# A list scheduler's cost table, the store of the gate rows and the loads of w_ada, changed together in a two-layer attention / DeltaNet step

## The chip, the cores and the metric

One NeuronCore of one Trainium2 chip runs the whole step. The metric is the device time of one execution in microseconds, taken as the median of several executions. The engines are called PE (matrix multiply), DVE, ACT and POOL (elementwise work) and SP (the engine that issues the DMAs of this kernel, all into one queue).

## What is computed

Two layers, each with 256 context tokens and 1024 latent tokens of width 1024, all in float32:

```
mod = silu(cond) @ w_ada + b_ada;  shift, scale, gate = split(mod, 3)
h   = rmsnorm(x) * (1 + scale) + shift
z   = h @ w_in                       # q, kv latents, k_pe, gates, q/k/v of DeltaNet, a, b
o_a = attention(q, k, v) * silu(g_a) # 8 heads, keys = tokens (+ 256 cached)
o_b = rmsnorm(delta_fwd + delta_bwd) * silu(g_b)  # 4 heads, chunked gated delta rule
x   = x + gate * (concat(o_a, o_b) @ w_out)
```

A final rmsnorm gives the outputs; the compressed keys, the rotary keys and the final DeltaNet states are outputs too. `gate` is one row of 1024 numbers for context tokens and one for latent tokens, in each layer.

## The kernel before

**Order of the work.** The kernel's Python code holds a planner, the class `Sched`. The work is written as some forty generators ("threads": projection weights, projection matmuls, evacuation, DeltaNet heads, attention heads, adaLN, output). Every instruction a thread asks for becomes an `Op` with an engine, a planned duration (`Eng.ns`, line 314) and the tiles that it reads and writes. `Sched.run` (line 104) always takes the op that could start first by its own clocks, and at equal time the thread with the lower number in `PR`. So the planner's durations decide the order of the instructions on each engine, and they decide nothing else: on the chip each engine runs its own list in that order, and a wait at the head of a list holds up all that is behind it. `keep_warm` (line 177) puts filler matmuls on the tile `spare` (line 406) into planned gaps of PE.

**What the planner believes.** A float32r matmul of n columns takes 0.4219 n ns (216.0 ns for 512), a plain float32 one four times that. The second and later of several matmuls into fewer than 65 partitions take 20 ns, and going back to a full-width matmul costs 85 ns. A DMA occupies SP for 450 ns, starts 1100 ns later, moves 360 bytes per ns, one DMA after the other, and its reader can start 931 ns after that (`LAT`, line 68; `Op.emit`, line 263).

**The w_ada pieces.** `ada` (line 452) makes one of the modulation vectors, half of it at a time: eight pieces of w_ada of 128 by 512, four matmuls with a two-column stationary operand each into `adap`, four copies into `msb`, a transpose into `modtp`, an add of the bias. The first four halves come from `init_thread`; the eight later ones (64 pieces of 256 KB) come from `ada_thread` (line 810), which loads each piece into the one buffer `wa` and then multiplies it, beside the layer-0 projection.

**The gate rows.** At the end of the two gate vectors (`s == 2 and half`, line 476) two DMAs write `modG` [128 partitions, 8] to the DRAM rows `gate_d[l, c]`, with the partition as the fastest index of the row: 1024 elements of 4 bytes each. `load_gate` (line 1675) reads the rows back much later, broadcast over partitions.

**The inverse of the DeltaNet chunks.** For each head `inv_thread` (line 1055) inverts the 32 by 32 diagonal blocks on DVE, writes them by four DMAs through `diag` (line 965; 1280 runs of 128 bytes each) into `wz_d` and `ai_d`, reads whole 128 by 128 blocks back into `wd` and `tt` (`rows`), and multiplies them on PE into `ph`.

**The seam of the two layers.** `mm_thread` makes the output projection tile by tile (ten tiles of 128 tokens); `fin(t)` (line 1679) stores the new x of a tile, normalises it, transposes it and splits it for layer 1 (`emit_h`, line 492).

Of the kernel before, what the change touches and what calls it, by code (L numbers as in the profile page):

```python
# [8 lines left out]
F32 = mybir.dt.float32  # L9
F32R = mybir.dt.float32r  # L10
# [4 lines left out]
DRAM = bass.MemoryType.DRAM  # L15

P = 128
DM = 1024
KD = DM // P
# [37 lines left out]
class Sched:  # L57
# [25 lines left out]
    half = False  # L83
# [135 lines left out]
class Op:  # L219
    def __init__(self, call, eng, ns, outs, ins):  # L220
        self.call, self.eng, self.ns = call, eng, ns
        self.outs, self.ins = [Sched.span(x) for x in outs], [Sched.span(x) for x in ins]
        self.thread = Sched.active
        self.half = outs[0].start_partition() if eng == "PE" and int(outs[0].shape[0]) <= 64 else None
        self.names = {n for n, _ in self.outs}
# [37 lines left out]
    def emit(self):  # L263
        s = self.start()
        if self.eng == "PE":
            if self.half:
                self.ns = 20
            elif Sched.half and self.half is None:
                s += 85
            Sched.half = self.half is not None  # L270
        e = s + self.ns
        if self.eng == "PE":
            Sched.keep_warm(s)
            Sched.busy.append((s, e))
        if self.eng == "D":
            e = Sched.bw = max(s + 1100, Sched.bw) + self.ns
        Sched.clk[self.eng] = s + 450 if self.eng == "D" else e
        e = int(e) * 8 + Sched.CODE[self.eng]
# [12 lines left out]


class Eng:
# [5 lines left out]
    def __getattr__(self, name):  # L299
        f = getattr(self.eng, name)  # L300

        def g(*a, **k):
            aps = [x for x in list(a[1:]) + list(k.values()) if hasattr(x, "start_partition")]
            acc = k.get("accum_out")
            outs = [a[0]] if acc is None else [a[0], acc]
            op = Op(lambda: f(*a, **k), self.key, self.ns(name, a, k, aps), outs, [x for x in aps if x is not acc])  # L306
            if Sched.active is None:
                op.emit()
            else:
                Sched.active.q.append(op)  # L310

        return g

    def ns(self, name, a, k, aps):
        size = lambda t: int(np.prod(t.shape[1:]))
        n = size(a[0])
        if self.key == "D":
            return int(np.prod(a[0].shape)) * 4 / 360
        if self.key == "PE":
            if name == "transpose":  # L320
                return 109
            if n == 1:
                return 214
            f = 0.4219 * (1 if a[2].dtype == F32R else 4)
            return f * max(n, min(int(a[1].shape[1]), 128))
# [42 lines left out]
def body(tc, I, O):  # L368
# [83 lines left out]
    def ada(l, s, half, load, msb):  # L452
# [23 lines left out]
        if s == 2 and half:  # L476
            for c in range(2):
                SY.dma_start(gate_d[l, c].rearrange("(k p) -> p k", p=P), modG[:, l, :, c])
# [49 lines left out]
    def mixer(l, hhl):  # L528
# [179 lines left out]
        def evac_conv(j, h, b, c0, n, ps):  # L708
# [11 lines left out]
            y = wp.tile([P, 520], F32, tag="yc", name="yc", bufs=2)[:, : e - a]  # L720
# [3 lines left out]
            th = wp.tile([P, 520], F32, tag="thc", name="thc", bufs=1)  # L724
# [85 lines left out]
        def ada_thread():  # L810
            yield "gdn"

            def load(l, k, c0):
                w = wp.tile([P, 512], F32, tag="wa", name="wa", bufs=1)
                SY.dma_start(w, I["w_ada"][l, k * P : (k + 1) * P, c0 : c0 + 512])
                yield 0
                return w

            msb = wp.tile([P, P], F32, tag="msb", name="msb", bufs=1)
            G.memset(msb, 0.0)  # L820
            for ll, s in ((0, 2), (1, 0), (1, 1), (1, 2)):
                for half in range(2):
                    yield from ada(ll, s, half, load, msb)
# [150 lines left out]
        def gram_thread(h):  # L974
# [24 lines left out]
            k2 = ap.tile([P, NT], F32, tag="k2", name="k2", bufs=3)  # L999
# [11 lines left out]
            n2 = ap.tile([P, NT], F32, tag="n2", name="n2", bufs=3)  # L1011
# [4 lines left out]
            bp = ap.tile([P, 2, NT], F32, tag="bp", name="bp", bufs=3)  # L1016
            kdb = ap.tile([P, 2, NT], F32, tag="kdb", name="kdb", bufs=3)
# [343 lines left out]
        def rope():  # L1361
# [6 lines left out]
            for g in range(2):  # L1368
                w = wp.tile([P, 520], F32, tag="thc", name="wpe", bufs=1)[:, 0:512].rearrange("p (a b) -> p a b", a=2)
                SY.dma_start(w, I["w_qpe"][l, g])  # L1370
                yield 0
                for b, (c0, n) in enumerate(BLK):
# [7 lines left out]
                    A = wp.tile([P, 520], F32, tag="yc", name="ra", bufs=2)[:, :n]  # L1380
                    if b == 0:
                        S.copy(A, pts[0][:, :n])
                    else:
                        B = wp.tile([P, 520], F32, tag="yc", name="rb_", bufs=2)[:, :n]
# [294 lines left out]
        def fin(t):  # L1679
# [3 lines left out]
            if l < DEPTH - 1:  # L1683
                if t in (0, 2, 6):
                    if t:
                        yield f"fin{t-1}"
                    alloc_h(*nxt)
# [169 lines left out]
```

## Time and profile before

| what | value |
|---|---|
| median of 3 runs | 2316.05 us (2313.68 to 2320.44) |
| the profiled execution's own time | 2314.35 us |
| its span, first to last instruction | 2312.4 us |
| granted PE clock, mean over the span | 0.976 |
| busy PE, DVE, ACT, POOL | 2123.5, 1461.7, 773.1, 830.1 us |
| moved by DMA | 306.9 MB in 369,808 packets, of which 92,624 under 512 bytes |

Busy time of PE counts the filler matmuls too. All instructions have the line of one helper (L306, the call of `Op`), so groups are told apart by their tiles: `ph<-wd,tt` is a matmul that reads `wd` and `tt` and writes `ph`. A plain float32 matmul stands in the profile as two records. The idle time behind an arrow is that of the engine just before the instruction, and the arrow names what ended it. The granted clock has two levels, 1.00 (2.4 GHz) and 0.50 (1.2 GHz).

### The profile page before, as it was taken

Reading aid. Unit: us, or ns where it says so; the run is one execution under the profiler, and the core shown is the slowest. Engines: PE = TensorE matmul, PEld = TensorE weight load, DVE = VectorE, ACT = ScalarE, POOL = GpSimd, SP = SyncE. Lnnn points to the kernel's source line nnn. Section 1 sums busy time; section 2 is a strip of 40 time slices with the busy share of each in tenths; the row PEclk is TensorE's granted clock in tenths of the full one; section 3 lists DMA queues with packets and bytes.
Section 4 is the critical chain, followed back from the end, with each engine's and each line's share of the span. In section 5 each row is a group of like instructions: output and inputs, shape, how many; then the busy total and the mean of one; then the engine's idle time right before and its main releaser. Section 6 shows DMA issues by size and latency. Waiting matters only on the chain. (4 is left out here: it accounts for less than half of the span.)

```text
span 2312.4 us, 35225 instructions
## 1 busy us (share of the span) xinstructions
PE 2123.5 (92%) x12230; PEld 1536.0 (66%) x12230; DVE 1461.7 (63%) x3085; ACT 773.1 (33%) x2118; POOL 830.1 (36%) x757
## 2 busy tenths in 40 slices
PE   8988998699988999999999899979988899999998
PEld 5666776578656654555777778867866666555576
DVE  5846367666775675654676556786767566565454
ACT  4242142323223445443222313331332234544311
POOL 2332123231523248355331421452152223844521
PEclk9999999899999999999999999999999999999999
DMA  7475666675844322101423545646685431310143
GB/s 264 129 188 140 194 199 192 141 219 149 273 137 123 99 87 68 27 23 39 151 97 96 154 141 158 184 137 194 188 240 154 119 88 50 102 45 23 39 151 109
DMA packets 369808, 306.90 MB, mean 133 GB/s; under 512 B 92624, under 2 KB 308112, under 8 KB 369376
## 3 DMA queue, kind: packets, MB, share of 16 engines
q1 hardware_dynamic: 369632, 304.66, 44.9%
q8 instruction: 97, 1.59, 0.3%
q14 instruction: 79, 0.65, 0.1%
HBM read 199.11 MB, written 105.46 MB: 132 GB/s over the span
## 5 line engine op out<-in xcount | busy, mean ns | idle before, releaser
L306 PE MATMUL zp<-hh,wh 128*128 128x512 f32 (+2 forms) x1128 | 425.5, 377 | 1.3 <-ACT qtp L306 0.9
L306 PE MATMUL zp<-hh,wl 128*128 128x512 f32 (+2 forms) x1128 | 421.4, 374 | 4.7 <-POOL wl L306 2.6
L306 PE MATMUL zp<-hl,wh 128*128 128x512 f32 (+2 forms) x1128 | 421.2, 373 | 2.7 <-POOL hl L306 1.5
L306 POOL TENSOR_TENSOR wl<-wr,wh 128x512 fp32r<-128x512 f32 (+1 forms) x114 | 158.7, 1393 | 399.3 <-DVE wh L306 247.1
L306 ACT ACTIVATE pe<-sp 128x512 f32<-128x512 f32 (+1 forms) x352 | 200.9, 577 | 246.0 <-PE sp L306 228.0
L306 DVE TENSOR_REDUCE at<-pm 128x1 f32<-128x512 f32 (+1 forms) x336 | 214.2, 682 | 103.9 <-PE pm L306 103.2
L306 POOL TENSOR_TENSOR pe<-pe,pe 128x1024 f32<-128x1024 f32 x96 | 229.8, 2394 | 90.2 <-DVE pe L306 64.7
L306 PE MATMUL sp<-at 97*128 97x512 f32 (+1 forms) x704 | 241.1, 408 | 1.4 <-ACT pe L306 0.9
L306 PEld LDWEIGHTS zp<-hh,wl 128*128 128x128 f32 (+1 forms) x1128 | 215.6, 191 | 37.8 <-issue 4.0
L306 PEld LDWEIGHTS zp<-hl,wh 128*128 128x128 f32 (+1 forms) x1128 | 215.7, 191 | 37.0 <-issue 4.3
L306 PEld LDWEIGHTS zp<-hh,wh 128*128 128x128 f32 (+1 forms) x1128 | 215.8, 191 | 36.2 <-issue 5.5
L306 PE MATMUL po<-pe,vv 128*64 128x512 f32 (+1 forms) x768 | 183.7, 561 | 3.2 <-ACT pe L306 2.4
L306 PEld LDWEIGHTS sp<-at 97*128 97x128 f32 x704 | 123.2, 190 | 89.1 <-issue 58.1
L306 POOL TENSOR_SCALAR kpt<-ktok,kdb 128x128 f32<-128x128 f32 x160 | 113.5, 722 | 91.6 <-DMA kp_d<-kpt 81.0
L306 PE MATMUL sp<-at,at 97*128 97x512 f32 (+1 forms) x352 | 137.9, 392 | 0.0
L306 PE MATMUL pm<-at 96*128 96x512 f32 (+1 forms) x416 | 128.0, 381 | 4.7 <-DMA ti<-ai_d 2.1
L306 DVE TENSOR_TENSOR pe<-pe,pe 128x256 f32<-128x256 f32 (+1 forms) x64 | 74.8, 1171 | 79.6 <-POOL pe L306 56.5
L306 PE MATMUL wop<-woh,oh 128*128 128x512 f32 x288 | 115.0, 399 | 0.9 <-DVE oh L306 0.9
L306 PE MATMUL wop<-woh,ol 128*128 128x512 f32 x288 | 114.1, 396 | 1.5 <-POOL ol L306 1.5
L306 PE MATMUL wop<-wol,oh 128*128 128x512 f32 x288 | 114.5, 398 | 0.0
L306 PEld LDWEIGHTS pm<-at 96*128 96x128 f32 x416 | 70.9, 189 | 58.4 <-ACT pe L306 17.9
L306 DVE TENSOR_TENSOR wtmp<-blk,W 104x31 f32<-104x31 f32 (+15 forms) x248 | 104.0, 419 | 7.0 <-POOL W L306 2.7
(264 smaller groups left out, 3895.1 us busy)
## 6 DMA issues: line engine op xcount, KB each, us to landing
wr<-in_w_main SPq DMA_DIRECT2D x116, 256.0 KB
ai_d<-ai SPq DMA_DIRECT2D x80, 256.0 KB
ti<-ai_d SPq DMA_DIRECT2D x160, 128.0 KB
wa<-in_w_ada SPq DMA_DIRECT2D x64, 256.0 KB
kqv_d<-yc SPq DMA_DIRECT2D x48, 256.5 KB
kq<-kqv_d SPq DMA_DIRECT2D x16, 641.0 KB
rb<-grow_d SPq DMA_DIRECT2D x80, 128.0 KB
kp_d<-kpt SPq DMA_DIRECT2D x80, 128.0 KB
```

Of the source, the lines that this page charges most:

```text
L306: op = Op(lambda: f(*a, **k), self.key, self.ns(name, a, k, aps), outs, [x for x in aps if x is not acc])
```

## The change

It gives the planner other durations: a float32r matmul 0.4545 ns per column (232.7 ns for 512), a plain float32 one 1.676; 92 ns for the change from full-width matmuls to ones with at most 64 output partitions and 200 ns back; 8 ns for a neighbour in the same bank; a DMA by its runs of contiguous bytes (`descriptors`), at 160 ns a run under 16 bytes and 8 + b/26 ns a run of b bytes otherwise (9 more under 512 bytes), divided by 16; and SP busy for at least one ns per run. The gate rows are transposed on PE and copied by ACT to 16 partitions of 128, and one DMA stores them. The later w_ada pieces are loaded by a thread of their own into two buffers, and the multiplying thread waits for flags. Small buffers lose a copy or six columns to make room. Each `fin(t)` waits for the one before it, where three did.

```diff
-                self.ns = 20
-            elif Sched.half and self.half is None:
-                s += 85
-            Sched.half = self.half is not None
+            n = self.outs[0][0]
+            if (self.half is None) != (Sched.half is None):
+                s = max(s, Sched.clk.get("PE", 0.0) + (92 if Sched.half is None else 200))
+            if self.half is not None:
+                if Sched.half not in (None, (n, self.half)) and Sched.half[0] == n:
+                    self.ns = 8
+            Sched.half = None if self.half is None else (n, self.half)
...
-        Sched.clk[self.eng] = s + 450 if self.eng == "D" else e
+        Sched.clk[self.eng] = s + self.issue if self.eng == "D" else e
...
+            if self.key == "D":
+                op.issue = max(450, self.descriptors(a[0], a[1])[0])
...
-            return int(np.prod(a[0].shape)) * 4 / 360
+            m, b = self.descriptors(a[0], a[1])
+            return m * (160 if b < 16 else 8 + b / 26 + (9 if b < 512 else 0)) / 16
...
-            f = 0.4219 * (1 if a[2].dtype == F32R else 4)
-            return f * max(n, min(int(a[1].shape[1]), 128))
+            if a[2].dtype == F32R:
+                return 0.4545 * max(n, 128)
+            if int(a[0].shape[0]) <= 32 and n < 128:
+                return 0.84 * n
+            return 1.676 * max(n, min(int(a[1].shape[1]), 128))
...
         if s == 2 and half:
-            for c in range(2):
-                SY.dma_start(gate_d[l, c].rearrange("(k p) -> p k", p=P), modG[:, l, :, c])
+            yield 0
+            pt = yield from bank("modtp")
+            PE.transpose(pt[0 : 2 * KD, 0:P], modG[:, l].rearrange("p k c -> p (k c)"), ident)
+            S.copy(msb[0 : 2 * KD, :], pt[0 : 2 * KD, 0:P])
+            free(pt)
+            SY.dma_start(gate_d[l].rearrange("c (k p) -> k c p", p=P), msb[0 : 2 * KD, :])
...
-            y = wp.tile([P, 520], F32, tag="yc", name="yc", bufs=2)[:, : e - a]
+            y = wp.tile([P, 514], F32, tag="yc", name="yc", bufs=2)[:, : e - a]
...
-            def load(l, k, c0):
-                w = wp.tile([P, 512], F32, tag="wa", name="wa", bufs=1)
-                SY.dma_start(w, I["w_ada"][l, k * P : (k + 1) * P, c0 : c0 + 512])
-                yield 0
-                return w
...
+            def loads():
+                for ll, s, half in jobs:
+                    for k in range(KD):
+                        i = len(wq)
+                        if i >= 2:
+                            yield f"au{i-2}"
+                        w = wp.tile([P, 512], F32, tag="wa", name="wa", bufs=2)
+                        c0 = s * DM + half * 512
+                        SY.dma_start(w, I["w_ada"][ll, k * P : (k + 1) * P, c0 : c0 + 512])
+                        wq.append(w)
+                        sd.flag(f"al{i}")
+                        yield 0
+
+            def get(l, k, c0):
+                nonlocal n
+                if n:
+                    sd.flag(f"au{n-1}")
+                yield f"al{n}"
+                n += 1
+                return wq[n - 1]
...
-            k2 = ap.tile([P, NT], F32, tag="k2", name="k2", bufs=3)
+            k2 = ap.tile([P, NT], F32, tag="k2", name="k2", bufs=2)
...
-            bp = ap.tile([P, 2, NT], F32, tag="bp", name="bp", bufs=3)
-            kdb = ap.tile([P, 2, NT], F32, tag="kdb", name="kdb", bufs=3)
+            bp = ap.tile([P, 2, NT], F32, tag="bp", name="bp", bufs=2)
+            kdb = ap.tile([P, 2, NT], F32, tag="kdb", name="kdb", bufs=2)
...
+                if t:
+                    yield f"fin{t-1}"
                 if t in (0, 2, 6):
-                    if t:
-                        yield f"fin{t-1}"
                     alloc_h(*nxt)
```

`descriptors(o, i)` finds the longest contiguous run on each side of the DMA and gives the number of runs and the bytes of one.

## Rows read from the trace of the kernel before

**Rows 1.** The page: the span, and the busy time of PE.

```profile
span 2312.4 us, 35225 instructions
PE 2123.5 (92%) x12230; PEld 1536.0 (66%) x12230; DVE 1461.7 (63%) x3085; ACT 773.1 (33%) x2118; POOL 830.1 (36%) x757
```

**Rows 2.** Waits of PE, whole span: total us, times, longest us.

```profile
PE ph L306 <- DMA tt<-ai_d: 47.7, 11, 12.2
PE adap L306 <- DMA wa<-in_w_ada: 16.8, 17, 2.0
...
PE ph L306 <- issue: 5.7, 4, 2.6
```

**Rows 3.** Timeline of SP, 158 to 182 us: start us, duration us.

```profile
163.88 1.74 SPq L306 DMA_DIRECT2D gate_d<-modG  x2
...
166.33 0.42 SPq L306 DMA_DIRECT2D wa<-in_w_ada  x1
...
171.44 7.13 SPq L306 DMA_DIRECT2D ai_d<-ai  x2
```

**Rows 4.** Timeline of PE, 158 to 182 us, idle before it in brackets.

```profile
177.82 0.61 PE L306 MATMUL adap<-wa,sc 128*2 128x128 f32 x8 [9.11 <-DVE ai L306]
```

**Rows 5.** Timelines of SP and of PE, 430 to 456 us.

```profile
442.87 0.51 SPq L306 DMA_DIRECT2D gate_d<-modG  x1
...
451.04 2.05 PE L306 MATMUL ph<-wd,tt 128*128 128x128 f32 x8 [12.20 <-DMA tt<-ai_d]
```

**Rows 6.** Windows, sum over two half-clock spells, 172.2 to 182.4 and 441.8 to 455.5.

```profile
sum 23.90, PE 9.04 PEld 6.85 DVE 5.06 ACT 0.62 POOL 2.42; mean PE 4.52 PEld 3.42 DVE 2.53 ACT 0.31 POOL 1.21
```

**Rows 7.** Windows, sum over seven half-clock spells that follow a wait of `ph`.

```profile
sum 40.80, PE 30.89 PEld 28.33 DVE 12.51 ACT 2.47 POOL 9.47; mean PE 4.41 PEld 4.05 DVE 1.79 ACT 0.35 POOL 1.35
```

**Rows 8.** Tile `mxt`: an existing transpose to few partitions, ns min/median/max.

```profile
L306 PE MATMUL mxt<-ident,at x16: 272/274/276, 705.8 to 2154.2; 128*10 128x128 f32 x16
```

**Rows 9.** Timeline of SP, 1550 to 1564 us: the diagonal stores and the loads behind them.

```profile
1549.69 2.07 SPq L306 DMA_DIRECT2D wz_d<-WP  x1
...
1557.11 0.42 SPq L306 DMA_DIRECT2D tt<-ai_d  x1
```

**Rows 10.** Timelines of PE around three of the waits of `ph`.

```profile
711.40 0.91 PE L306 MATMUL ph<-wd,tt 128*128 128x128 f32 x3 [4.25 <-DMA tt<-ai_d]
...
1562.24 2.05 PE L306 MATMUL ph<-wd,tt 128*128 128x128 f32 x8 [8.93 <-DMA tt<-ai_d]
...
1824.04 2.05 PE L306 MATMUL ph<-wd,tt 128*128 128x128 f32 x8 [7.15 <-DMA tt<-ai_d]
```

**Rows 11.** Windows: length, then busy PE, PEld, DVE, ACT, POOL, clock, DMA.

```profile
696.00:754.00 58.00, 49.30 (x355) 36.37 (x355) 31.68 (x69) 20.78 (x53) 18.58 (x16) 0.94 0.49 132
...
986.00:1044.00 58.00, 57.44 (x261) 31.70 (x261) 33.84 (x51) 25.98 (x49) 29.10 (x17) 1.00 0.09 22
...
1798.00:1856.00 58.00, 47.64 (x349) 34.87 (x347) 27.00 (x71) 19.65 (x48) 19.00 (x14) 0.94 0.40 106
```

**Rows 12.** Windows of the filler matmuls (tile `spare`) alone: busy PE, PEld.

```profile
1770.00:1830.00 60.00, 13.81 (x110) 13.17 (x110) 0.94 0.36 92
```

**Rows 13.** Tile `wa`: the 64 loads, duration ns, first and last start.

```profile
L306 SPq DMA_DIRECT2D wa<-in_w_ada x64: 327/346/1961, 87.7 to 424.6; - x64
```

**Rows 14.** Timeline of SP, 88 to 125 us.

```profile
92.39 0.33 SPq L306 DMA_DIRECT2D wa<-in_w_ada  x1
```

**Rows 15.** Timeline of PE, 88 to 125 us.

```profile
87.64 0.39 PE L306 MATMUL zp<-hh,wh 128*128 128x512 f32 x1
...
88.80 0.39 PE L306 MATMUL zp<-hh,wl 128*128 128x512 f32 x1
...
95.76 0.40 PE L306 MATMUL adap<-wa,sc 128*2 128x128 f32 x8
```

**Rows 16.** The seam: tile `xn` on DVE, and the timeline of POOL.

```profile
L306 DVE TENSOR_SCALAR xn<-x,rs x9: 752/753/754, 1103.1 to 1216.8; 128x1024 f32<-128x1024 f32 x9
...
1109.52 1.29 POOL L306 TENSOR_TENSOR hl<-hf,hh 128x512 fp32r<-128x512 f32 x1 [6.46 <-DVE hh L306]
```

More of the change, by code (lines that the diff above doesn't have):

```diff
@@ L82 @@
     seq = 0
-    half = False
+    half = None
     psum = set()
@@ L224, in __init__ @@
         self.half = outs[0].start_partition() if eng == "PE" and int(outs[0].shape[0]) <= 64 else None
+        self.issue = 450
         self.names = {n for n, _ in self.outs}
@@ L265, in emit @@
         if self.eng == "PE":
-            if self.half:
-                self.ns = 20
-            elif Sched.half and self.half is None:
-                s += 85
-            Sched.half = self.half is not None
+            n = self.outs[0][0]
[5 more added lines that the diff above has]
+            Sched.half = None if self.half is None else (n, self.half)
         e = s + self.ns
@@ L312, in __getattr__, with descriptors @@
         return g
+    @staticmethod
+    def descriptors(o, i):
+        runs = []
+        for x in (o, i):
+            r = 1
+            for a, b in reversed([(int(a), int(b)) for a, b in x.ap][0 if x.space == DRAM else 1 :]):
+                if a != r and b != 1:
+                    break
+                r *= b
+            runs.append(r)
+        n = int(np.prod(o.shape))
+        r = min(*runs, n)
+        return n // r, 4 * r
     def ns(self, name, a, k, aps):
@@ L723, in evac_conv @@
             V.scalar_tensor_tensor(y, in0=zp[:, a + 2 : e + 2], scalar=cw[:, 2:3], in1=y, op0=ALU.mult, op1=ALU.add)
-            th = wp.tile([P, 520], F32, tag="thc", name="thc", bufs=1)
+            th = wp.tile([P, 514], F32, tag="thc", name="thc", bufs=1)
             S.activation(th[:, : e - a], y, AF.Tanh)
@@ L811, in ada_thread @@
             yield "gdn"
-            def load(l, k, c0):
-                w = wp.tile([P, 512], F32, tag="wa", name="wa", bufs=1)
-                SY.dma_start(w, I["w_ada"][l, k * P : (k + 1) * P, c0 : c0 + 512])
-                yield 0
-                return w
             msb = wp.tile([P, P], F32, tag="msb", name="msb", bufs=1)
             G.memset(msb, 0.0)
-            for ll, s in ((0, 2), (1, 0), (1, 1), (1, 2)):
-                for half in range(2):
-                    yield from ada(ll, s, half, load, msb)
+            jobs = [(ll, s, half) for ll, s in ((0, 2), (1, 0), (1, 1), (1, 2)) for half in range(2)]
+            wq, n = [], 0
+            def loads():
[17 more added lines that the diff above has]
+                return wq[n - 1]
+            sd.add(PR['ada'], loads())
+            for ll, s, half in jobs:
+                yield from ada(ll, s, half, get, msb)
             sd.flag("ada")
@@ L1010, in gram_thread @@
             yield 0
-            n2 = ap.tile([P, NT], F32, tag="n2", name="n2", bufs=3)
+            n2 = ap.tile([P, NT], F32, tag="n2", name="n2", bufs=2)
             V.tensor_scalar(n2, k2, EPS, None, op0=ALU.add)
@@ L1368, in rope @@
             for g in range(2):
-                w = wp.tile([P, 520], F32, tag="thc", name="wpe", bufs=1)[:, 0:512].rearrange("p (a b) -> p a b", a=2)
+                w = wp.tile([P, 514], F32, tag="thc", name="wpe", bufs=1)[:, 0:512].rearrange("p (a b) -> p a b", a=2)
                 SY.dma_start(w, I["w_qpe"][l, g])
@@ L1379, in rope @@
                         yield 0
-                    A = wp.tile([P, 520], F32, tag="yc", name="ra", bufs=2)[:, :n]
+                    A = wp.tile([P, 514], F32, tag="yc", name="ra", bufs=2)[:, :n]
                     if b == 0:
@@ L1383, in rope @@
                     else:
-                        B = wp.tile([P, 520], F32, tag="yc", name="rb_", bufs=2)[:, :n]
+                        B = wp.tile([P, 514], F32, tag="yc", name="rb_", bufs=2)[:, :n]
                         V.tensor_tensor(A, pts[0][:, :n], cs_[:, c0 - SEQ : c0 - SEQ + n], op=ALU.mult)
```

## The prediction

> **What bounds the kernel now.** I read the page first. PE is busy for 2123.5 of 2312.4 us and no other engine for more than 63% [rows 1]: what can be won is PE's 188.9 us of idle time, and what a halved clock costs. Then the waits of PE, longest sum first: `ph` waits 47.7 us for the load of `tt`, in 11 waits, and 5.7 us more with no releaser shown; `adap` waits 16.8 us for `wa` in 17 waits [rows 2]. Then the two timelines around the two longest waits. At 163.88 SP issues the two gate stores and at 166.33 the next load of `wa`; the two stores of `ai` behind it hold SP for 7.13 us [rows 3]. The next matmul of PE reads that `wa` and starts after 9.11 idle us [rows 4]; its arrow names DVE, but what it needs is the load. At 442.87 another gate store goes out, and PE stands 12.20 us for `tt` [rows 5]. Last the windows with the granted clock: after such stops PE works at 0.50, the 1.2 GHz level, for a few us. Two spells of that kind stand behind the gate stores, with 9.04 busy us of PE in them [rows 6], and seven more behind waits of `ph` (from 233.6, 564.7, 711.5, 1366.8, 1558.0, 1718.4 and 1820.8), with 30.89 [rows 7]; half of that busy time is the price.
>
> The sum is made against the profiled execution, 2314.35 us (2 us beside its span), which is 1.7 us under the median. About 0.3%, 7 us, is what a measurement here can tell from no change.
>
> **1. The gate rows: 19 us less.** Four DMAs of 1024 elements of 4 bytes go, two DMAs of 16 rows of 512 bytes come, so the stops behind them go. The first is 9.11 us [rows 4]. The second is 12.20 us [rows 5], of which a plain wait for `tt` would have stayed: the other ten average (47.7 - 12.2) / 10 = 3.55 us [rows 2], which leaves 8.65. The clock: 9.04 / 2 = 4.5 us lost [rows 6], less one spell of the ordinary kind, 30.89 / 2 / 7 = 2.2 [rows 7], is 2.3. Added are two transposes with 16 output rows; the kernel has one with 10, of 274 ns [rows 8], and with a change of tiling I put 0.5 us for each. The ACT copies and stores lie beside other work: the rows are read only in the layer's last stage. 9.1 + 8.65 + 2.3 - 1 = 19. Bounds: 9 (the first stop alone) and 23.
>
> **2. The DMAs of the inverse priced by their runs: 34 us less.** Each of the four diagonal stores is 1280 runs of 128 bytes. The planner before gave each 455 ns (163,840 bytes / 360) and the new one 1280 x 21.9 / 16 = 1754 ns, so it expects `tt` 4 x 1.3 = 5.2 us later and puts other matmuls in front of `ph`. That this is the right size the trace tells: SP needs 2.07 us to issue one of them, `tt` is issued 7.4 us after it [rows 9], and the ordinary waits of PE are 3.55 us. Ten of those and the rest of the one behind the gate store are 39.05 us. From this I take off what 5.2 us doesn't cover (8.93 - 5.2 = 3.7, [rows 10]) and two waits of 4.25 and 7.15 us [rows 10] that lie where PE has nothing else to do: from 696 to 754 and from 1798 to 1856 it is busy for only 49.30 and 47.64 of 58 us [rows 11], and in the 60 us from 1770 on 13.81 of its busy time is filler [rows 12]. That leaves 24 us. Elsewhere the projection's matmuls fill the gap. Four or five spells of slow clock at 2.2 us go with them: 10 us. The 5.7 us without a releaser I leave. Bounds: 0 (the moved matmuls are missed later) and 39 + 5.7 + 17.6 = 62 us.
>
> **3. Two buffers for w_ada: 6 us less.** The 64 loads go out from 87.7 to 424.6, one per 5.3 us [rows 13]. The planner reckons 1100 + 728 + 931 ns = 2.76 us from issue to use, after the change 2.73; measured it is 95.76 - 92.39 = 3.4 us [rows 14, 15]. So the plan stays 0.6 us short, and the multiplying thread, which has the better priority, will still be put where the plan has the load arrive. But with two buffers loads come in pairs, so 32 arrivals instead of 64 can be late: half of 16.8 is 8.4, less 2 for loads that now stand closer together. What is late next is then the other piece of a pair. Bounds: all 16.8 gone, or every pair late by 1 us, 32 in place of 16.8, which is 15 us more.
>
> The Trainium skill ("DMA: Bandwidth & Descriptors", the section on the anatomy of one DMA on the gpsimd path) fits a transfer as 2.0 us plus bytes at 436 GB/s. That would be 2.6 us for a piece, the plan would be long enough, all waits would go and the sum would be 11 us lower. The measured 3.4 us, on SP's queue, disagrees, and it decides.
>
> **4. PE's own price: 9 us more.** Five projection matmuls start (88.80 - 87.64) / 5 = 232 ns apart [rows 15]. The planner had 216.0 and now has 232.7. Its order was thus made for a PE 7% faster than the real one, so each result of another engine that it thought just in time was a little early. That margin goes. Waits of PE other than those named above are 188.9 - 47.7 - 5.7 - 16.8 - 9.1 = 109.6 us; 8% more is 9. Bounds: 15 us less (a plan that is true also orders better) and 60 us more (rival D).
>
> The Trainium skill ("TensorE: Matmul & The Clock Gate", the section on the back-to-back issue gap) gives n / 2.4 + 2.5 ns at full clock, 216 ns for 512 columns, which is the figure that this change throws out. By that rule the new plan would think PE slower than it is, all other engines would have more margin and this term would be 0, the sum 9 us lower. The rows at granted clock 1.00 have 232, so the trace speaks against it.
>
> **5. Nothing for the rest.** The chain of `fin`: from `xn` at 1103.1 to the end of POOL's `hl` at 1110.8 it takes 7.7 us, and a tile comes every (1216.8 - 1103.1) / 9 = 12.6 us [rows 16]. So the tile's matmuls hide each added wait; were they gone, it would cost up to 7.7 us a tile. The store of x queued behind it is read in the next layer's last stage only. The smaller `k2`, `n2`, `bp`, `kdb`: head h already waits for the scan of head h-2, so a second copy is free in time; without that cover a head would wait for the gram of the one before. The six columns were unused.
>
> Sum: 2314.35 - 19 - 34 - 6 + 9 = 2264.35, and 1.7 up to the median: **2266 us**. Its own range by the likelier parts of the bounds: 2235 to 2290.
>
> **Rivals.**
> A. *Everything falls in place.* With a true PE price and true DMA prices the waits on DVE, ACT and POOL shrink too: half of all idle time goes (94 us), and half of the 20 us of slow clock in [rows 6, 7] with it: 2316 - 94 - 10 = 2212. For it: many of the 109.6 us are waits below 2 us that order alone could fill. Against: prices of those engines don't change.
> B. *The filling runs out.* What is put in front of `ph` is missed in the poor stretches [rows 11, 12], which grow by the same time; parts 2 to 4 sum to nothing and only the gate rows pay: 2316 - 19 = 2297. For it: PE already runs filler there. Against: after them the attention stage is full (57.44 of 58 us from 986 on, [rows 11]), and what starts it would come sooner too.
> C. *The change doesn't do what it says.* SP was held at 171.44 by its own two stores of 256 KB, not by the small elements, so the stops stay; the reordering is a wash: 2316.
> D. *The margin was worth more than the truth*, the slower case. All waits for the other engines sit in the 109.6 us; parts 1 to 3 give 59, so it decides from the point where these waits grow by more than 54%. At 80% more they cost 88: 2316 - 59 + 88 = 2345. Place: the hand-overs of the scan (`up` on `ru`) and of attention. Against: in attention PE is full [rows 11], and there the other engines wait for it.
>
> **How the numbers follow.** Forecast 0.60, A 0.08, B 0.17, C 0.06, D 0.09. Faster by over 0.3%: forecast, A and B, 0.85; same: C, 0.06; slower: D, 0.09. The range 2212 to 2309 holds the forecast, B and about half of A; it leaves out C, D and the rest of A, some 0.2.
>
> **What would show it.** Right: two stores of the gate rows instead of four, no store of `ai` that holds SP for 7 us, no wait of PE over 8 us; `ph` waits for `tt` under 20 us in sum; the last `wa` load well before 424; a granted clock above 0.976. Wrong: `ph` still waiting 40 us (part 2), a longer sum of `adap` waits (part 3), more filler in the poor stretches (B), or `up`, `otp`, `pd` waits that doubled (D).

## The result, and the profile after

The changed kernel takes 2328.27 us in the median (2326.39 to 2332.94, 4 runs) against 2315.21 (2313.68 to 2320.44, 4 runs): a ratio of 1.0055 [1.0033, 1.0078], 13 us slower. The forecast was 2266 us, 50 us faster.

The page of the changed kernel (span, PE, DMA packets), to be held against [rows 1] and the table ahead of it:

```profile
span 2324.6 us, 35790 instructions
PE 2160.3 (93%) x12502; PEld 1570.9 (68%) x12502; DVE 1464.2 (63%) x3085; ACT 778.3 (33%) x2120; POOL 832.8 (36%) x757
DMA packets 365699, 306.95 MB, mean 132 GB/s; under 512 B 88480, under 2 KB 304000, under 8 KB 365264
```

PE's idle time fell, from 188.9 to 164.3 us, and the kernel is longer all the same: PE is busy 36.8 us more. The filler matmuls say with what (tile `spare`; before there were 440 records):

```profile
L430 PE MATMUL spare<-ident x710: 271/275/583, 3.2 to 2134.7; 128*128 128x128 f32 x178
```

and their busy time over the whole span (before it was 62.43 us):

```profile
sum 2324.00, PE 96.60 PEld 89.24; mean PE 19.32 PEld 17.85
```

The waits of PE (total us, times, longest us), against [rows 2]:

```profile
PE vtp L309 <- DMA vt<-kqv_d: 11.6, 5, 4.0
PE up L309 <- DVE ru L309: 10.8, 15, 1.5
PE ph L309 <- DMA tt<-ai_d: 10.1, 13, 2.5
PE adap L309 <- DMA wa<-in_w_ada: 9.9, 13, 2.4
...
PE pd L309 <- DVE pe L309: 9.2, 5, 4.9
...
PE pd L309 <- DVE at L309: 6.8, 1, 6.8
```

`ph` for `tt` went from 47.7 to 10.1 us, `adap` for `wa` from 16.8 to 9.9. The gate stores on SP (start, duration), against [rows 3, 5]:

```profile
130.13 0.79 SPq L309 DMA_DIRECT2D gate_d<-msb  x1
131.03 3.55 SPq L309 DMA_DIRECT2D wa<-in_w_ada  x3
...
264.91 0.69 SPq L309 DMA_DIRECT2D gate_d<-msb  x1
```

There are two stores instead of four and no hold of 7 us behind them, and PE's waits of 9.11 and 12.20 us are gone: its longest is now 6.8 us. The time is lost elsewhere. The windows of the first projection and around the start of the two attention stages, first of before, all of PE and then the filler alone (length, then busy PE, PEld, ..., clock, DMA):

```profile
0.00:640.00 640.00, 563.87 (x3899) 438.96 (x3900) 398.86 (x966) 198.79 (x641) 190.43 (x243) 0.96 0.66 190
640.00:960.00 320.00, 293.42 (x1598) 185.56 (x1597) 214.82 (x415) 130.08 (x304) 133.07 (x91) 0.97 0.32 93
...
1700.00:2110.00 410.00, 380.76 (x2109) 241.75 (x2108) 264.30 (x534) 160.45 (x384) 171.42 (x132) 0.98 0.35 100
...
0.00:640.00 640.00, 24.62 (x154) 21.73 (x154) 0.96 0.66 190
640.00:960.00 320.00, 12.09 (x90) 10.84 (x90) 0.97 0.32 93
...
1700.00:2110.00 410.00, 22.45 (x172) 20.78 (x172) 0.98 0.35 100
```

and of the changed kernel:

```profile
0.00:640.00 640.00, 580.39 (x3955) 448.26 (x3957) 397.84 (x975) 201.70 (x645) 201.04 (x244) 0.97 0.63 193
640.00:960.00 320.00, 298.41 (x1739) 197.36 (x1736) 208.13 (x412) 129.58 (x301) 129.27 (x91) 0.98 0.30 87
...
1700.00:2110.00 410.00, 377.91 (x2032) 243.76 (x2030) 262.16 (x498) 153.85 (x350) 173.21 (x127) 0.96 0.32 93
...
0.00:640.00 640.00, 25.18 (x162) 22.46 (x162) 0.97 0.63 193
640.00:960.00 320.00, 32.62 (x268) 31.03 (x268) 0.98 0.30 87
...
1700.00:2110.00 410.00, 28.49 (x200) 26.29 (x200) 0.96 0.32 93
```

The length, less PE's busy time, plus the filler's, is the time in which PE did nothing useful. Around the two starts of attention it was before (320 - 293.42 + 12.09) + (410 - 380.76 + 22.45) = 90.4 us, after 54.2 + 60.6 = 114.8. The page alone would hide this, since filler counts as busy. The timeline of PE at the start of the first attention stage of the changed kernel shows how it looks:

```profile
695.13 4.41 PE L430 MATMUL spare<-ident 128*128 128x128 f32 x38
700.04 0.28 PE L309 MATMUL mxt<-ident,at 128*10 128x128 f32 x1 [0.50 <-DVE at L309]
700.15 2.40 PE L430 MATMUL spare<-ident 128*128 128x128 f32 x20
702.77 0.85 PE L309 MATMUL otp<-ident,oT 128*128 128x128 f32 x6 [0.22 <-DVE oT L309]
703.45 8.43 PE L430 MATMUL spare<-ident 128*128 128x128 f32 x74
712.91 1.13 PE L309 MATMUL ph<-wd,tt 128*128 128x128 f32 x8 [1.03 <-DMA tt<-ai_d]
```

No wait here is longer than 1.03 us, but 17.8 us lie between 695.13 and 712.91 and 1.1 of them do work. By the rule of `keep_warm`, filler is put only where the plan itself has a gap: the planner expected the late `tt` and had no other matmul to put there. The layer's projection ended at 639 us, and attention hasn't opened.

### The profile page after: what moved, and what is told of

The parts are those of the page before. It is cut to its first block, busy times and chain, and to the rows that moved or that the text cites. A ratio compares the mean times of both kernels' runs of the same rounds, so it can differ in the third digit from the quotient of the medians.

```text
span 2324.6 us, 35790 instructions
## 1 busy us (share of the span) xinstructions
PE 2160.3 (93%) x12502; PEld 1570.9 (68%) x12502; DVE 1464.2 (63%) x3085; ACT 778.3 (33%) x2120; POOL 832.8 (36%) x757
## 3 DMA queue, kind: packets, MB, share of 16 engines
q1 hardware_dynamic: 365520, 304.66, 43.5%
## 5 line engine op out<-in xcount | busy, mean ns | idle before, releaser
L309 POOL TENSOR_TENSOR pe<-pe,pe 128x1024 f32<-128x1024 f32 x96 | 231.5, 2411 | 80.9 <-DVE pe L309 40.8
L309 POOL TENSOR_SCALAR kpt<-ktok,kdb 128x128 f32<-128x128 f32 x160 | 120.5, 765 | 96.8 <-DMA kp_d<-kpt 78.1
L309 DVE TENSOR_TENSOR pe<-pe,pe 128x256 f32<-128x256 f32 (+1 forms) x64 | 85.1, 1330 | 102.4 <-POOL pe L309 52.1
L309 PE MATMUL pm<-at 96*128 96x512 f32 (+1 forms) x416 | 123.2, 380 | 2.1 <-DVE at L309 1.1
L309 DVE TENSOR_TENSOR wtmp<-blk,W 104x31 f32<-104x31 f32 (+15 forms) x248 | 96.5, 389 | 21.2 <-POOL W L309 17.5
```

## The experiments

All ratios are against the kernel before, run beside each experiment (its medians go from 2315 to 2319 us), with a 95% interval. Ratios and not times are compared across runs, 0.001 being 2.3 us. In the cuts of code, `...` marks lines left out.

**e1, the kernel before with the new store of the gate rows alone.**

```diff
-                SY.dma_start(gate_d[l, c].rearrange("(k p) -> p k", p=P), modG[:, l, :, c])
...
+            PE.transpose(pt[0 : 2 * KD, 0:P], modG[:, l].rearrange("p k c -> p (k c)"), ident)
+            S.copy(msb[0 : 2 * KD, :], pt[0 : 2 * KD, 0:P])
...
+            SY.dma_start(gate_d[l].rearrange("c (k p) -> k c p", p=P), msb[0 : 2 * KD, :])
```

> The kernel before with the new store of the gate rows alone (transpose, copy, one store of 16 rows in each layer's turn). All theories: the two stops of PE of 9.1 and 12.2 us go. Theory of the prediction (a stop removed is time won): 2316 - 19 = about 2297. Theory of the start (the start of attention in each layer hangs on a chain of its own: last projections, rotary part, row maxima on DVE, store of the maxima through SP; time won before it comes back as idle time or filler of PE): 2310 to 2317, the first sp matmul of layer 0 less than 5 us before 718. Theory of the lottery (any change of the plan reshuffles the order, worth some 10 us either way): anything from 2300 to 2330, without a link to the stops.

2307.48 us, 0.9947 [0.9928, 0.9965]: the part wins 12 us by itself, between what the two theories expected. The theory of the start is out, since the first `sp` comes at 709.6, 9 us sooner. The two stores of `ai` that held SP for 7.13 us behind the gate store in [rows 3] hold it for 1.26 here:

```profile
168.78 1.26 SPq L306 DMA_DIRECT2D ai_d<-ai  x2
```

**e2, the changed kernel with all PE prices of before.**

```diff
-                return 0.4545 * max(n, 128)
...
-            return 1.676 * max(n, min(int(a[1].shape[1]), 128))
+            f = 0.4219 * (1 if a[2].dtype == F32R else 4)
+            return f * max(n, min(int(a[1].shape[1]), 128))
```

and the tiling costs back to 20 ns for a neighbour and 85 ns for the return.

> The changed kernel with the planner's PE prices and tiling costs of before (0.4219 ns per column, 20 and 85 ns), all else as changed. Rival D of the prediction (the margin of the low PE price was worth more than the truth): it falls below the kernel before, to some 2290 to 2305, and the waits of PE on DVE, ACT and POOL shrink. Theory of the start: it stays within 7 us of 2315 to 2328. Lottery: anything from 2300 to 2335.

2290.61 us, 0.9887 [0.9846, 0.9927], where rival D had it: the new PE prices cost 1.0055 - 0.9887, or 39 us. With the old ones the rest of the change wins 26 us (17 to 36 by the interval), and not the 59 of parts 1 to 3.

**e3, the changed kernel with the DMA price of before.**

```diff
-            return m * (160 if b < 16 else 8 + b / 26 + (9 if b < 512 else 0)) / 16
+            return int(np.prod(a[0].shape)) * 4 / 360
```

and 450 ns of SP for every DMA again.

> The changed kernel with the planner's DMA prices of before (360 bytes per ns, SP for 450 ns), all else as changed. All theories: the waits of ph for tt come back, some 35 to 45 us in sum instead of 10. Theory of the prediction (a stop removed is time won): it gets slower than the changed kernel by 20 to 34 us, 2348 to 2362. Theory of the start: no more than 10 us from 2328, and the filler matmuls fall back towards 220. Lottery: anything from 2310 to 2345.

2347.79 us, 1.0118 [1.0088, 1.0148]: the new DMA price is worth 15 us, less than the 20 to 34 that the theory of the prediction gave. The waits for `tt` do come back. PE's wait in this run, its span and busy time, and the busy time of the filler (tile `spare`, whole span):

```profile
PE ph L309 <- DMA tt<-ai_d: 55.2, 13, 12.3
...
span 2338.4 us, 35067 instructions
PE 2123.8 (91%) x12116; PEld 1540.3 (66%) x12116; DVE 1463.4 (63%) x3085; ACT 775.5 (33%) x2120; POOL 833.0 (36%) x757
...
sum 2338.40, PE 48.01 PEld 42.07; mean PE 48.01 PEld 42.07
```

But the time in which PE does nothing useful is the same: 2338.4 - 2123.8 + 48.0 = 262.6 us here, and 2324.6 - 2160.3 + 96.6 = 260.9 with the new price. From 0 to 640 and from 960 to 1700 us the new price saves 35 us of it; from 640 to 960 and from 1700 to 2110 us it gives back 33. So the 45 us of waits that it fills are paid for at other places, most of them around the starts of attention, and its gain must come from somewhere else (see the end of this section).

**e4, the changed kernel with one buffer for w_ada and no thread for its loads.**

```diff
-                        w = wp.tile([P, 512], F32, tag="wa", name="wa", bufs=2)
...
+                w = wp.tile([P, 512], F32, tag="wa", name="wa", bufs=1)
```

> The changed kernel with the one buffer for the w_ada pieces and no thread of its own for the loads, all else as changed; the pieces last until some 430 us again instead of 262. Theory of the prediction: 6 us slower, 2334. Theory of the start: the pieces were something that PE could do later, so with one buffer more of them is left for later and less filler is needed; same or up to 6 us faster, 2320 to 2328. Lottery: anything from 2310 to 2340.

2329.2 us, 1.0043 [1.0024, 1.0061]: no difference from the changed kernel that these intervals show, though `adap` waits 22.8 us here in place of 9.9:

```profile
PE adap L309 <- DMA wa<-in_w_ada: 22.8, 21, 4.6
```

**e5 to e8, which PE price it is.** e5 takes the changed kernel with the rate of before, e6 with the tiling costs of before and the new rate, e7 goes further down with the rate, e8 moves it by half a per cent to see whether the order is a matter of luck.

```diff
-                return 0.4545 * max(n, 128)
+                return 0.4219 * max(n, 128)
...
+                return 0.39 * max(n, 128)
...
+                return 0.457 * max(n, 128)
```

and for e6:

```diff
-                s = max(s, Sched.clk.get("PE", 0.0) + (92 if Sched.half is None else 200))
...
+            if self.half:
+                self.ns = 20
+            elif Sched.half and self.half is None:
+                s += 85
```

> The changed kernel with one number back: the planner prices a float32r matmul at 0.4219 ns per column again; the new tiling costs and the new price of plain float32 matmuls stay. Margin theory (rival D: a PE priced 7% too cheap puts more projection matmuls in front of every matmul that waits for another engine): like the run with all PE prices old, 2283 to 2300, last projection matmul of layer 0 before 625, first sp of layer 0 before 690. Tiling theory (the 92 and 200 ns of the tiling change did the harm): like the changed kernel, 2320 to 2335. Lottery: anywhere from 2285 to 2335.

> The changed kernel with the tiling costs of before (20 and 85 ns), the price of 0.4545 ns per column stays. Margin theory: like the changed kernel, 2318 to 2335, last projection matmul of layer 0 after 630. Tiling theory: 2285 to 2300. Lottery: anywhere from 2285 to 2335.

> The changed kernel with a float32r matmul priced at 0.39 ns per column, 16% below what the trace shows (232 ns per 512). Margin theory: as fast as with 0.4219 or faster, 2270 to 2295, fewer and shorter waits of PE on other engines. Theory of the prediction (the truer the plan the better the order): slower than both 0.4219 and 0.4545. Lottery: anywhere from 2285 to 2335.

> The changed kernel with a float32r matmul priced at 0.4570 in place of 0.4545 ns per column, half a per cent more: nothing but a nudge. Margin theory: within 7 us of the changed kernel's 2328. Lottery: off by 10 us or more, up or down, with the milestones of the layers moved as much as the larger edits move them.

e5 2283.64 us, 0.9848 [0.9832, 0.9865]; e6 2265.24, 0.9769 [0.9742, 0.9796]; e7 2278.37, 0.9829 [0.9812, 0.9847]; e8 2330.32, 1.0054 [1.0034, 1.0075]. Beside e2 this makes a table of four:

| | tiling costs of before | new tiling costs |
|---|---|---|
| rate of before (0.4219) | 0.9887 (e2) | 0.9848 (e5) |
| new rate (0.4545) | 0.9769 (e6) | 1.0055 (changed kernel) |

With the old tiling costs the new rate wins 27 us (e6 keeps the new prices of plain float32 matmuls too, which were not tried by themselves). With the old rate the new tiling costs change nothing that the intervals show. Only the two together do harm, 48 us over e5 and 66 over e6, and a small step doesn't change that (e8). e5, e7 and e8 lie where the margin theory had them, but e5 without its two signs: the last projection matmul of layer 0 comes at 632 and the first `sp` at 702. e6 lies under all three ranges, and the margin theory had it at 2318 or more. (0.39 is 14% below 0.4545, and not the 16 of the expectation.) e6 is the fastest version of all, 54 us under the kernel before. Its windows, all of PE and the filler:

```profile
640.00:960.00 320.00, 306.76 (x1709) 191.59 (x1706) 218.63 (x414) 139.40 (x325) 137.84 (x91) 1.00 0.29 83
1700.00:2110.00 410.00, 392.10 (x2154) 245.03 (x2154) 265.80 (x504) 173.92 (x385) 181.04 (x122) 1.00 0.28 79
...
640.00:960.00 320.00, 15.09 (x124) 14.40 (x124) 1.00 0.29 83
1700.00:2110.00 410.00, 22.87 (x184) 21.66 (x184) 1.00 0.28 79
```

28.3 + 40.8 = 69.1 us without useful work in place of 114.8: 45.7 of the 65.3 us between the two spans lie here, and the granted clock of both stretches is 1.00 instead of 0.98 and 0.96. A hole of the same kind stands ahead of attention here too, with 10 us of filler in place of 15.

**e9 to e12, is it the sum?** What a block of small matmuls really costs can be read in the attention stage of the changed kernel:

```profile
1002.36 0.39 PE L309 MATMUL sp<-at,at 97*128 97x512 f32 x1
1002.68 1.08 PE L309 MATMUL po<-pe,vv 128*64 128x512 f32 x4
1003.69 0.97 PE L309 MATMUL pm<-at 96*128 96x512 f32 x4
...
1005.97 1.08 PE L309 MATMUL po<-pe,vv 128*64 128x512 f32 x4
```

The first `po` starts 0.32 us after the last `sp`, 0.09 more than the 232 ns of [rows 15]; the next full-width matmul follows 1.01 us later, for 858 + 8 planned, so the way back would be 143 ns and not 200. (That is an estimate: 858 and 8 are the planner's prices.) e9 puts 143; e10 leaves the tiling costs of before and makes the rate too high; e12 does that with the new ones; e11 lets the change of tiling count as busy time in the filler rule.

```diff
-                s = max(s, Sched.clk.get("PE", 0.0) + (92 if Sched.half is None else 200))
+                s = max(s, Sched.clk.get("PE", 0.0) + (92 if Sched.half is None else 143))
...
-                return 0.4545 * max(n, 128)
+                return 0.49 * max(n, 128)
...
+                c = Sched.clk.get("PE", 0.0)
+                Sched.clk["PE"] = c + (92 if Sched.half is None else 200)
...
+                Sched.busy.append((c, Sched.clk["PE"]))
```

> The changed kernel with 143 ns in place of 200 for going back to a full-width matmul: in the trace of before, two po matmuls of 858 ns keep PE for 1.01 us until the next full-width matmul starts, so 1010 - 858 - 8 = 143. Theory T (rate and tiling together make the planned PE slower than the real one in attention, so results of other engines are planned too late and PE's list is poorly filled): the surplus of 57 ns for each of some 370 blocks goes, and the time comes down by a third of the 63 us between the changed kernel and the one with the old tiling costs or more: 2290 to 2308. Theory C (the size of the price does not matter, any such list lies where chance puts it): anything from 2265 to 2330, no more likely low than high. Theory F (tiling costs open planned gaps, which fill with filler matmuls): smaller gaps, a few filler matmuls fewer, 2315 to 2328.

> The changed kernel with the tiling costs of before (20 and 85 ns) and a rate of 0.49 ns a column, 8% above the measured 0.4545. Theory T: the planned PE is slower than the real one everywhere, and the time is as bad as the changed kernel's or worse, 2315 to 2340. Theory F: it is the tiling costs that hurt, not the sum, so it stays near the 2265 of the true rate with the old tiling costs: 2255 to 2285. Theory C: anything from 2260 to 2330.

> The changed kernel, all prices as they are, but the 92 and 200 ns count as busy time of PE for the planner's filler rule and not as idle time. Theory F: the filler matmuls fall from 710 records by 100 or more, and 20 us or more of the 63 come back: 2265 to 2308. Theory T: what is planned when stays as it was, only some filler goes, whose place idle time takes: 2318 to 2330. Theory C: the same as T, because filler does not take part in the choice of the next instruction.

> The changed kernel with a rate of 0.49 in place of 0.4545, tiling costs as changed. Theory T: the time goes on rising as the plan gets slower (2278 at 0.39, 2284 at 0.4219, 2328 at 0.4545): 2330 to 2370. Theory F: as the changed kernel, 2315 to 2335. Theory C: anything from 2270 to 2340.

e9 2304.75 us, 0.9949 [0.9927, 0.9970]; e10 2314.18, 0.9980 [0.9963, 0.9996]; e11 2330.24, 1.0049 [1.0031, 1.0067]; e12 2345.15, 1.0115 [1.0086, 1.0144]. e9, e10 and e12 are outside theory F's ranges, so it falls; e11 itself tests it little, since it took away only 40 of the 710 filler records. e9 and e12 lie where theory T has them. e10 is just under T's range, and 17 us faster than the changed kernel where T had it as slow or slower. Theory C's ranges hold e9, e10 and, at the edge, e11; e12 is above them. To put all prices on one scale, take the step of the stage shown above, 1002.68 to 1005.97, 3.29 us: one block of `po` with both changes, 1.10, and so (3.29 - 1.10) / 0.2327 = 9.4 full matmuls. The plan has for it 9.4 x 512 x rate and the block by its tiling costs (1158 ns new, 1101 in e9, 963 or 969 with the old ones):

| run | rate, tiling costs | plan of the step, us | against 3.29 | ratio to before |
|---|---|---|---|---|
| e2 | 0.4219, old | 3.00 | -8.8% | 0.9887 |
| e7 | 0.39, new | 3.03 | -7.7% | 0.9829 |
| e15 | 0.44, old | 3.08 | -6.3% | 0.9875 |
| e6 | 0.4545, old | 3.15 | -4.2% | 0.9769 |
| e5 | 0.4219, new | 3.19 | -3.0% | 0.9848 |
| e9 | 0.4545, return 143 | 3.29 | 0.0% | 0.9949 |
| e10 | 0.49, old | 3.32 | +1.0% | 0.9980 |
| changed kernel | 0.4545, new | 3.35 | +1.8% | 1.0055 |
| e8 | 0.457, new | 3.36 | +2.1% | 1.0054 |
| e12 | 0.49, new | 3.52 | +6.9% | 1.0115 |

Where the planned PE is 3 to 9% faster than the real one, the ratios lie between 0.977 and 0.989; at the true price and above it they lie between 0.995 and 1.012. That the ten part so speaks against chance alone (theory C). But the scale was made when the ten times were known, from one step of full attention, and among the first five runs it orders nothing: it describes where the harm begins, and doesn't say by which wait.

**e13 to e15, is it the margin of the engines that feed PE?** e13 is the changed kernel with DVE, ACT and POOL 8% dearer, e14 the same with 143 ns for the return, e15 the step between 0.4219 and 0.4545 with the old tiling costs (in the table).

```diff
-            return 51 + 0.8333 * n + 93 * ptr + 42 * (aps[0].space != PSUM)
+            return 1.08 * (51 + 0.8333 * n + 93 * ptr + 42 * (aps[0].space != PSUM))
...
```

> The changed kernel, its PE and DMA prices kept, with all planned durations of DVE, ACT and POOL 8% higher. Theory M (the planner must think PE faster, relative to the engines that feed it, than it is, so that their results are planned with a margin): the ratio of the prices is then about that of the run with the rate of 0.4219 and the new tiling costs (2284), and the time falls to 2265 to 2300. Theory P (PE's price against DMAs and the fixed delays between engines is what counts, the durations of DVE, ACT and POOL don't): 2315 to 2335. Theory C (chance): anything from 2265 to 2335.

> As the run before it, with 143 ns for going back to a full-width matmul, so that PE's prices are all as measured. Theory M: truth for PE and a margin at the other engines together, 2250 to 2285. Theory P: as the run with 143 ns alone, 2295 to 2312.

> The changed kernel with the tiling costs of before and a rate of 0.44, between 0.4219 (2291) and 0.4545 (2265). Theory M: the bottom of the curve is flat within some 15 us, 2255 to 2290. Theory C: anything from 2255 to 2330, half of it above 2290.

e13 2319.53 us, 1.0002 [0.9985, 1.0019]; e14 2314.85, 0.9991 [0.9972, 1.0011]; e15 2285.82, 0.9875 [0.9853, 0.9897]. Theory M falls: e13 gives back 12 us of the 66 between the changed kernel and e6, and e14 is slower than e9, its like without the dearer engines. Theory P (PE's price against the DMAs and the fixed delays is what counts) has e13 in its range and misses e14 by 3 us; no run tried it by itself. e15 is within theory M's range, but 25 us above e6, so the bottom of the curve isn't flat within 15 us.

**e16 and e17, attention opened first.** The preparation of head 0 and its row maxima go ahead of the DeltaNet threads, in the changed kernel and in e6.

```diff
-PR = dict(... prep0=3, ... red0=3, ...)
+PR = dict(... prep0=1.5, ... red0=1.5, ...)
```

> The changed kernel, all prices kept, with the preparation of attention head 0 and its row maxima ahead of the DeltaNet threads (prep0 and red0 at 1.5 in place of 3). Theory S (with dear PE prices many instructions could start at the same planned time, the thread order decides, and it puts the DeltaNet tail ahead of what opens attention, so PE stands there without either): the first sp comes before 705 instead of at 717, the idle and filler time of PE from 640 to 960 and 1700 to 2110 falls from 108 to 80 or less, and the time to 2275 to 2305. Theory E (the prices act through the order everywhere, the start of attention is only where it shows): the first sp comes sooner, the DeltaNet tail later by as much, 2315 to 2335.

> The same two thread numbers in the changed kernel with the tiling costs of before, the fastest so far (2265). Theory S: attention opens in time there already, so little changes, 2255 to 2275. Theory E: a moved order without a gain, 2260 to 2300.

e16 2313.8 us, 0.9977 [0.9954, 1.0001]; e17 2282.38, 0.9853 [0.9810, 0.9896]. The first `sp` of the kernel before, of e2, of the changed kernel, of e6 and of e16, one row of each (duration min/median/max, then first and last start):

```profile
L306 PE MATMUL sp<-at x704: 278/396/797, 718.3 to 2186.8; 97*128 97x512 f32 x160, 97*128 97x256 f32 x16
```

```profile
L307 PE MATMUL sp<-at x704: 277/395/774, 656.6 to 2158.1; 97*128 97x512 f32 x160, 97*128 97x256 f32 x16
```

```profile
L309 PE MATMUL sp<-at x704: 274/395/796, 716.6 to 2195.4; 97*128 97x512 f32 x160, 97*128 97x256 f32 x16
```

```profile
L307 PE MATMUL sp<-at x704: 277/395/505, 701.2 to 2133.9; 97*128 97x512 f32 x160, 97*128 97x256 f32 x16
```

```profile
L309 PE MATMUL sp<-at x704: 274/395/796, 692.2 to 2180.9; 97*128 97x512 f32 x160, 97*128 97x256 f32 x16
```

The windows of e16, all of PE and the filler:

```profile
640.00:960.00 320.00, 297.12 (x1678) 191.69 (x1677) 211.40 (x420) 128.88 (x305) 128.36 (x87) 0.98 0.32 92
1700.00:2110.00 410.00, 381.85 (x2023) 240.02 (x2021) 274.19 (x520) 160.40 (x364) 182.53 (x133) 0.97 0.33 96
...
640.00:960.00 320.00, 19.77 (x156) 18.52 (x156) 0.98 0.32 92
1700.00:2110.00 410.00, 12.84 (x90) 11.83 (x90) 0.97 0.33 96
```

Attention opens 24 us sooner in e16 than in the changed kernel, and the time without useful work in the two windows falls from 114.8 to 83.6 us. Of these 31 us only 18 reach the end (1.0055 to 0.9977), between what the two theories expected; e17 is 19 us slower than e6, as theory E had it. How early attention opens doesn't order the runs: the changed kernel opens it 2 us sooner than the kernel before, and e2, 45 us sooner than e6, is 27 us slower than e6. The start of attention is thus a place where the loss shows, and not the whole cause.

**Where the time of eight runs lies.** From one profile of each: PE's idle time, the filler, their sum, and what the half clock took from useful matmuls. The last is an estimate: the span is cut into windows of 2 us, and in each of them half of PE's useful busy time is counted for the share at 0.50. All in us.

| kernel | span | idle | filler | no useful work | half clock | rest |
|---|---|---|---|---|---|---|
| before | 2312.4 | 188.9 | 62.4 | 251.3 | 36.5 | 2024.6 |
| changed | 2324.6 | 164.3 | 96.6 | 260.9 | 39.1 | 2024.6 |
| e1, gate rows alone | 2307.3 | 173.7 | 65.3 | 239.0 | 44.5 | 2023.8 |
| e2, old PE prices | 2289.4 | 132.5 | 96.1 | 228.6 | 31.7 | 2029.1 |
| e3, old DMA price | 2338.4 | 214.6 | 48.0 | 262.6 | 49.9 | 2025.9 |
| e6, new rate, old tiling costs | 2259.3 | 130.7 | 85.0 | 215.7 | 20.3 | 2023.3 |
| e13, other engines dearer | 2316.8 | 149.8 | 113.4 | 263.2 | 25.0 | 2028.6 |
| e16, attention first | 2306.9 | 161.0 | 69.0 | 230.0 | 48.6 | 2028.3 |

The rest is nearly the same in all (in all 19 traces it lies between 2016 and 2035 us), so to within 6 us the two columns before it are what one of these eight is slower or faster by. With one profile of each, a few us can be chance. The new PE prices cost 32 us of the first kind against e2, 26 of them in the two windows around the starts of attention. The new DMA price saves 2 us of the first kind and 11 of the second. e13 wins its time at the clock alone, with no less time without useful work than the changed kernel, which speaks against theory M once more. And e16 loses 10 of its 31 us at the clock and 4 in the rest.

## Why the prediction was wrong

**The step that failed is part 4**, PE's own price: forecast 9 us more, measured 39 (e2, some 30 to 48 by its interval). The term counted the rate alone, 216.0 against 232.7 ns, as 8% on 109.6 us of other waits. It put the new tiling costs at nothing without a reason. The runs have it otherwise: the new rate without them is 27 us faster (e2 to e6) and not 9 slower, and the loss comes only when both are there, 66 us from e6 to the changed kernel. That 39 lies inside the bounds given there (-15 to +60) is no credit to the working: the upper one is rival D's, whose reason isn't borne out (below). The term also looked for the price in waits, when half of it stands in the trace as filler: outside `ph` for `tt`, `adap` and the 9.1 us stop, idle time rose from 115 (109.6 + 5.7) to 164.3 - 10.1 - 9.9 = 144 us, and the filler's busy time by 34 (62.4 to 96.6 over the whole span).

Part 4 is half of the miss. The other half is that **parts 1 to 3 gave 26 us and not 59** (e2 against the kernel before): 33 us too much was forecast there and 30 too little in part 4, which but for rounding is the miss of 62 us (2266 to 2328). Neither half alone would have made the kernel slower: 59 - 39 and 26 - 9 are both gains.

**Part 1** was right in kind: 12 us (e1) for 19, within the bounds of 9 and 23. What was too high is the second stop: the sum of the waits for `tt` falls by 4.2 us in e1 (47.7 to 43.5), and not by 8.65. The two added transposes have no wait behind them.

**Part 2** filled the waits as forecast: under 20 us were expected, 10.1 are left, and with the old price they are 55.2 (e3). But it is worth 15 us and not 34, and not for the reason given. Its 24 us of waits came to 2, because the time came back elsewhere as idle time and filler; its 10 us of slow clock came true, as 11. The lower bound had named this: "the moved matmuls are missed later". One reading of its rows was also too narrow: of the four diagonal stores only two hold SP for some 2 us (`wz_d<-WP` and `ai_d<-W`, 2.1 and 1.8 us in the median of eight); the other two take 0.3 us.

**Part 3** was too high: waits of `adap` fell from 16.8 to 9.9 us, and the last `wa` load starts at 258.7 instead of 424.6, but the time with one buffer is the same (e4). Where the waits' 7 us went was not tried apart. The 3.4 us of [rows 14, 15] is the time until use and only an upper bound for the load, since PE didn't wait for that piece. That 2.6 us are too short is shown by a later one that it did wait for, issued at 108.79 and used at 112.77.

**Part 5** was not tried by itself, and the sum of the others doesn't test it, since prices that act together can't be added. The 14 us that remain of e2's gain without part 1 are near the 15 of the DMA price alone, so no loss is seen. (Before the change two of the ten `fin` waited, those of t = 2 and 6, and not three.)

**The rivals.** B named the place (the poor stretches after the projection) and gave the sign by which it goes; its row of filler came true, 12.1 to 32.6 us in the first of them. For the waits of part 2 e3 shows its mechanism. D named the price ("the margin was worth more than the truth") and was given 0.09. What came is D's price in B's place, at 13 us, short of D's 29. That 115 us of waits and filler grew by 29 + 34 us, 55%, near the 54% of D's turning point, is chance: that point was set against 59 us of gain, which were 26. Of D's signs only the waits of `pd` doubled (6.1 to 16.0 us); those of `up` and `otp` fell. Its reason, that results of DVE, ACT and POOL come late once the margin goes, isn't borne out, since a margin put back at those engines leaves the time without useful work as it was (263.2 us in e13 and 261.5 in e14, against 260.9). A is out, and so is C, since the stops went with the gate rows alone (e1). The Trainium skill ("TensorE: Matmul & The Clock Gate", the section on the back-to-back issue gap) gives 216 ns as the gap of a single matmul of 512 columns. Five in a row stand 232 ns apart in [rows 15], and by these the prediction rightly went. That a plan with a PE too slow would leave others more margin and cost nothing, as the prediction worked out beside that rule, is the opposite of what the runs show.

**What stays open** is by which choices of the planner the rate and the tiling costs, harmless apart, together leave PE without work around the starts of attention. That with dear matmuls more threads are ready at the same planned time, and the thread numbers then decide, fits e16 in part and was not shown by itself.

## What to carry to other kernels

In a planner that only fixes an order, a truer price is not a better one by itself, and two prices that do no harm alone can do it together: change one at a time, and then both. In this kernel the sum of a typical step did best a few per cent under its measured length; other kernels were not tried. Before a plan is judged by idle time, add the filler to it, by stage, and then what the half clock takes. A wait that is filled early has to be paid where no independent work is left, so look first at that stretch.

## What the runs showed of the hardware

A block of two `po` matmuls into 64 output partitions started 0.09 us later than a full-width matmul would have (0.32 us after the last `sp`, for 0.232), and the next full-width matmul followed 1.01 us after it, though the plan has each of the two at 0.86: the two halves ran side by side. Split by the planner's prices, the way back took 0.14 us, an estimate. And DVE was slower while POOL worked on 96 by 512 elements; POOL, then DVE, in the changed kernel:

```profile
660.16 2.64 POOL L309 TENSOR_TENSOR at<-at,at 96x512 fp32r<-96x512 f32 x2 [3.09 <-ACT at L309]
```

```profile
659.81 0.38 DVE L309 TENSOR_TENSOR wtmp<-blk,W 104x220 f32<-104x220 f32 x1
660.22 1.46 DVE L309 TENSOR_TENSOR W<-W,wtmp 104x220 f32<-104x220 f32 x1
661.71 1.35 DVE L309 TENSOR_TENSOR wtmp<-blk,W 104x231 f32<-104x231 f32 x1
```

Two operations whose likes take 0.38 and 0.39 us (the first of these rows, and the same `W` of 231 columns at 663.51) take 1.46 and 1.35 while POOL's pair runs. No run tried the one without the other. No price of either kernel knows that.
